# Three square weight products take their weight sums from DRAM, made earlier, and load their weights a turn at a time

## The chip, the cores and the metric

One Trainium2 chip, one core of it. The time is device microseconds (us) of one execution; the median over the runs shown is the number to predict. Engines are TensorE (PE, its weight loads PEld), VectorE (DVE), ScalarE (ACT), GpSimd (POOL) and SyncE (SP), whose queue issues nearly all DMA transfers in the order in which they stand in the program.

## What is computed

One layer of an encoder on 1024 prompt and 64 sample tokens, width 1024, all in float32, cut to its steps:

```python
h  = ffn_half(x, g_ffn1, w_ffn1_gu, w_ffn1_d)
u, q, k, v = split(rmsnorm(h, g_mix) @ w_in)       # input projection
y_ssm = s5_mixer(u, ...)                           # state space scans
y_att = diff_attn(q, k, v, ...)
h  = h + concat(y_ssm, y_att) @ w_out              # square, 1024 x 1024
mk, mv = rmsnorm(mem) @ w_ck, rmsnorm(mem) @ w_cv
q  = rmsnorm(h, g_cross) @ w_cq                    # square
h  = h + softmax_attention(q, mk, mv) @ w_co       # square
y  = rmsnorm(ffn_half(h, g_ffn2, ...), g_final)
```

The new keys, values and states are outputs as well.

## The kernel before

Matrix products run as three TensorE products of a high and a low part (line 171): ScalarE makes the high part `wh` of a 128 x 512 weight tile (line 151) and a copy `q` in PSUM (152), VectorE the low part `wl` (153).

The three square products with `w_out`, `w_cq` and `w_co` (in this order) are done as a two by two block product with seven block multiplications in place of eight (Strassen's scheme in Winograd's form). A `Block` holds one such product, `square` runs it in seven turns, in the order `TURNS = (0, 1, 3, 4, 5, 2, 6)`. A turn is 96 matmuls of 272 columns into eight banks. While turn n runs on TensorE, `prepare` gets the operands of turn n+1 ready, four times (k = 0 to 3): the split of a weight tile, a difference of activations (`value`, lines 422 and 426), and their split (450 on ScalarE, 451 on VectorE). Turns 0, 1 and 5 multiply by blocks of the weight as they are; turns 3, 4, 2 and 6 by sums and differences of blocks, which GpSimd makes in place out of the loaded blocks: three operations of 128 x 512 in `mix` (lines 433, 434, 435) for each k, and one more in `prepare` (448):

```python
G.tensor_tensor(out=s1, in0=a21, in1=a22, op=ALU.add)
G.tensor_tensor(out=a21, in0=a11, in1=a21, op=ALU.subtract)
G.tensor_tensor(out=a11, in0=a22, in1=a21, op=ALU.subtract)
```

The same class serves the down projections of the two feed-forward parts, with five more blocks.

The input projection (about 760 to 1050 us of the span) computes twelve units of 128 columns of `w_in`. The first four feed the scans `s5_main(f, u)`, which are written as generators, put into a list `bg` and moved on one step at a time as the later units are issued (`pump_all` moves each generator of the list by one step). A scan stores its input (line 1201), loads it back in another shape (1206), runs some 160 small VectorE operations (lines 1230 to 1262: products, sums and copies of two SBUF operands, 4 to 136 elements a partition), loads its two constants and its states (1268, 1270, 1271), and feeds TensorE again (1280, 1281) and a gelu on ScalarE (1282). ScalarE's line 1338 copies key or value heads to token order.

The order of every engine's instructions is set when the program is built: the framework keeps the program order of what each engine is given, weighted by priority and by the moment at which a simulated timeline has the operands ready. Tiles come from rotating pools: `row` (36 buffers, "r"), `wr` and `ws` (`half`), four buffers each, and seven of `wh` and `wl`.

Of the kernel before, what the change touches and what calls it, by code (L numbers as in the profile page):

```python
# [10 lines left out]
F32 = mybir.dt.float32  # L11
# [3 lines left out]
ALU = mybir.AluOpType  # L15
AX = mybir.AxisListType

P = 128
# [50 lines left out]
def tile_hymba_step(ctx: ExitStack, tc: tile.TileContext, a, o):  # L69
# [9 lines left out]
    wp = ctx.enter_context(tc.tile_pool(name="wp", bufs=7))  # L79
# [26 lines left out]
    def dram(shape, name):  # L106
        return dr.tile(list(shape), F32, tag=name, name=name)

    bg = deque()
# [29 lines left out]
    def half(shape=(P, 512), dt=F32):  # L139
        return wp.tile(list(shape), dt, tag="ws", name=nm("ws"), bufs=4)  # L140
# [101 lines left out]
    class Stats:  # L242


        def __init__(self):
            self.acc = None
# [132 lines left out]
    class Block:  # L379
# [11 lines left out]
        def load(self, part, k):  # L391

            n, held = self.n, self.held
            if k >= n:
                return
            j = k + (n if part > 1 else 0)
            wj = self.w_src(j)
            if part % 2 == 0:
                u = self.u[j] = held("u", k + 2 * part, row)
                load(out=u, in_=self.u_src(j))  # L400
            elif part == 1:
                self.a11[k] = held("a11", k, lambda: wp.tile([P, 512], F32, tag="wr", name=nm("wr"), bufs=4))
                self.a21[k] = held("a21", k // 2, lambda: row([P, 2, 512]))[:, k % 2]
                halves = (wj[:, 512:1024], wj[:, 0:512]) if self.swap else (wj[:, 0:512], wj[:, 512:1024])
                load(out=self.a11[k], in_=halves[0])
                load(out=self.a21[k], in_=halves[1])
            else:
                both = held("both", k, lambda: row([P, 2, 512]))
                self.a12[k], self.a22[k] = both[:, 0], both[:, 1]
                if self.swap:  # L410
                    for c in range(2):
                        load(out=both[:, c], in_=wj[:, 512 - 512 * c:1024 - 512 * c])
                else:
                    load(out=both, in_=wj.rearrange("p (c m) -> p c m", c=2))

        def value(self, q, k, late):

# [19 lines left out]
        def prepare(self, q, k, late=False):  # L437
            held = self.held
            if k == 0:
                held.turn[1] += 1  # L440
            if k >= self.n:
                return
            if self.s1[k] is None and q:
                self.mix(k)
            w = (self.a11[k], self.a12[k], self.s1[k], self.a11[k], self.a21[k], self.a22[k], self.a12[k])[q]
            self.w[q, k] = held.split_w(w)
            if q == 1:
                G.tensor_tensor(out=w, in0=w, in1=self.a11[k], op=ALU.subtract)
            v, r = self.value(q, k, late), held("x", 4 * (held.turn[1] % 2) + k, lambda: row([P, 2, HT], F32R))
            A.copy(r[:, 0], v)  # L450
            V.tensor_tensor(out=r[:, 1], in0=v, in1=r[:, 0].bitcast(F32), op=ALU.subtract)  # L451
            self.x[q, k] = r

        def product(self, q, i):

            p = [bank(), bank()]
            items = []
            for k in range(self.n):
                (wh, wl), r = self.w[q, k], self.x[q, k]
                items.append((wh[:, i * P:(i + 1) * P], wl[:, i * P:(i + 1) * P], r[:, 0], r[:, 1]))  # L460
            mm3(p, items, self.n, HC)
            return p

    TURNS = (0, 1, 3, 4, 5, 2, 6)

# [2 lines left out]
    def square(d, outs, done, step=lambda n, i: None, src_d=None):  # L468
# [19 lines left out]
        for n, q in enumerate(TURNS):  # L488
            for i in range(4):
                if q != 1:  # L490
                    residual(q, i)
                p = d.product(q, i)
                g, u = outs[i], outs[4 + i]
# [15 lines left out]
                step(n, i)  # L509
                if n < 6:  # L510
                    d.prepare(TURNS[n + 1], i, True)
                if n in (0, 2, 3, 4):
                    fetch((1, None, 5, 6, 2)[n], i)

# [831 lines left out]
    for f in range(4):  # L1346
        u = in_unit(f, True)
        pump_all()
        bg.append(s5_main(f, u))
    kT, qT, vt, vsr = [], [], [], row([NS, 4, P])  # L1350
    for hd in range(4):
        k = in_unit(8 + hd)
# [288 lines left out]
            if m % 8 == 7:  # L1641
                bg.append(subln(heads[m // 8]))

    def weights_of(w):
        return lambda k: w[k * P:(k + 1) * P]

    def begin(d):
        for k in range(4):
            d.load(1, k)
        for k in range(4):  # L1650
            d.prepare(0, k)
        for k in range(4):
            d.load(3, k)


    h2_d = dram([KT, P, NT], "h2_d")
# [40 lines left out]
    _, mv = mem_proj(a["w_cv"][0], "mem_v_prompt")  # L1697
    for t in range(2):
        store(out=mv_d[t], in_=mv[t])
    d = Block(Held(), 4, weights_of(a["w_out"][0]), cat)  # L1700
    begin(d)
    pump(1000)

# [72 lines left out]
    q = deque()  # L1776
# [9 lines left out]
                q.append(c_scores(0, i - 4 + C_EARLY))  # L1786

    bg.append(cache_prep())
    d = Block(Held(), 4, weights_of(a["w_cq"][0]), h2, swap=True)
    begin(d)  # L1790
    square(d, cq[4:] + cq[:4], lambda m, c: None, cq_step)
    pump(1000)
# [57 lines left out]
                c_values(*q.popleft())  # L1850
    while q:
        c_values(*q.popleft())
    d = Block(Held(), 4, weights_of(a["w_co"][0]), oc)
    begin(d)
    h3_d, h3 = dram([KT, P, NT], "h3_d"), [row() for _ in range(KT)]
    norm3 = Normed(h3, g_ffn2)
# [122 lines left out]
```

## Time and profile before

| | us |
|---|---|
| median of three runs | 2416.04 |
| lowest, highest | 2413.63, 2422.79 |
| the profiled execution | 2419.82 |
| its span | 2418.0 |
| PE busy | 2266.6 (94%) |
| PEld busy | 2200.5 (91%) |
| DVE busy | 1667.8 (69%) |
| ACT busy | 1308.6 (54%) |
| POOL busy | 1096.5 (45%) |
| moved by DMA | 262.64 MB |

TensorE is busy 94% of the span: the time is its work and its stalls. A busy TensorE does not run at its peak at all times: the granted clock is 1.2 GHz instead of 2.4 GHz in some short stretches, and an instruction takes twice as long there. The stages have different limits, so the questions of this change are read from two stages: the input projection with the scans, and the square products.

### The profile page before, as it was taken

What the parts mean: (1) busy time and instruction counts of PE and PEld (TensorE: products, weight loads), DVE (VectorE), ACT (ScalarE), POOL (GpSimd) and SP (SyncE); (2) the same over time, 40 slices, a digit from 0 to 9 for tenths busy, and PEclk for the clock granted to TensorE, in tenths of its full rate; (3) what the DMA queues carried; (4) which work ended last, traced back from release to release, by engine and by line L of the source; (5) the groups of instructions that cost most, each with busy time, mean ns of one, the idle gap of its engine ahead of it and who ended that gap; (6) DMA issues with size and microseconds to landing.
All of it is one profiled execution on the core that took longest, in us unless ns stands there. A gap on an engine that the chain in (4) does not pass through costs nothing. (4 is left out here: it accounts for less than half of the span.)

```text
span 2418.0 us, 45389 instructions
## 1 busy us (share of the span) xinstructions
PE 2266.6 (94%) x16914; PEld 2200.5 (91%) x16914; DVE 1667.8 (69%) x3732; ACT 1308.6 (54%) x2538; POOL 1096.5 (45%) x823
## 2 busy tenths in 40 slices
PE   6899999999999997989999899988999999998998
PEld 6799999998999997977799899888999999998997
DVE  6557543358898697259978678787654544479897
ACT  6554445446545422258856767666655444564543
POOL 2666777744144300025434420356776666644340
PEclk9999999999999998999999999999999999999999
DMA  6232444443412435533353411133232222262312
GB/s 210 71 113 81 112 114 119 118 169 144 144 40 84 145 90 142 161 122 97 108 179 125 155 62 47 61 111 98 81 99 72 75 78 81 78 221 85 115 46 92
DMA packets 267239, 262.64 MB, mean 109 GB/s; under 512 B 36445, under 2 KB 216714, under 8 KB 267018
## 3 DMA queue, kind: packets, MB, share of 16 engines
q1 hardware_dynamic: 266928, 259.72, 33.9%
q8 instruction: 133, 2.18, 0.4%
q14 instruction: 88, 0.72, 0.1%
q10 hardware_dynamic: 90, 0.02, 0.0%
HBM read 186.51 MB, written 68.58 MB: 105 GB/s over the span
## 5 line engine op out<-in xcount | busy, mean ns | idle before, releaser
L171 PE MATMUL b<-r,wh 128*128 128x272 f32 (+4 forms) x9600 | 1689.0, 296 | 68.7 <-DVE r L724 22.5
L171 PEld LDWEIGHTS b<-r,wh 128*128 128x128 f32 x9600 | 1420.9, 191 | 86.1 <-DVE r L724 26.7
L171 PE MATMUL b<-r,wl 128*128 128x272 f32 (+4 forms) x4800 | 1054.9, 295 | 23.6 <-DVE wl L153 23.6
L171 PEld LDWEIGHTS b<-r,wl 128*128 128x128 f32 x4800 | 784.6, 191 | 27.5 <-DVE wl L153 27.3
L596 DVE TENSOR_TENSOR r<-b,r 128x272 f32<-128x272 f32 x440 | 172.1, 433 | 253.2 <-PE b L171 229.1
L152 ACT CAST q<-wr 128x512 fp32r<-128x512 f32 x304 | 180.0, 592 | 269.1 <-DVE wl L153 267.0
L153 DVE TENSOR_TENSOR wl<-wr,q 128x512 fp32r<-128x512 f32 x304 | 206.8, 680 | 169.3 <-issue 69.9
L151 ACT CAST wh<-wr 128x512 fp32r<-128x512 f32 x304 | 187.9, 622 | 239.8 <-PE b L171 212.4
L451 DVE TENSOR_TENSOR r<-r,r 128x544 fp32r<-128x544 f32 x224 | 214.0, 973 | 23.9 <-ACT r L450 23.3
L433 POOL TENSOR_TENSOR ws<-r,r 128x512 f32<-128x512 f32 x32 | 54.2, 1700 | 304.4 <-DVE ws L1799 124.6
L151 ACT CAST wh<-ws 128x512 fp32r<-128x512 f32 x158 | 98.0, 620 | 134.6 <-PE b L171 113.9
L153 DVE TENSOR_TENSOR wl<-ws,q 128x512 fp32r<-128x512 f32 x158 | 107.5, 680 | 88.1 <-PE b L171 52.8
L152 ACT CAST q<-r 128x512 fp32r<-128x512 f32 x146 | 86.6, 593 | 124.5 <-DVE wl L153 124.2
L450 ACT CAST r<-r 128x544 fp32r<-128x544 f32 x224 | 144.2, 652 | 9.2 <-DMA r<-hid_d 7.6
L724 DVE SCALAR_TENSOR_TENSOR r<-b,r 128x272 f32<-128x272 f32 (+4 forms) x328 | 132.2, 437 | 21.9 <-PE b L171 20.9
L152 ACT CAST q<-ws 128x512 fp32r<-128x512 f32 x158 | 93.7, 593 | 87.1 <-DVE wl L153 82.3
L646 POOL TENSOR_TENSOR r<-r,r 128x544 f32<-128x544 f32 x44 | 61.5, 1398 | 171.7 <-DVE r L596 128.4
L1398 POOL CAST r<-r 64x256 fp32r<-64x256 f32 x32 | 13.6, 424 | 252.1 <-PE b L137 239.7
L153 DVE TENSOR_TENSOR wl<-r,q 128x512 fp32r<-128x512 f32 x146 | 99.4, 681 | 38.1 <-ACT q L152 37.1
L659 POOL TENSOR_TENSOR r<-r,r 128x1088 f32<-128x1088 f32 x44 | 111.8, 2543 | 8.8 <-ACT r L658 8.8
L137 PE MATMUL b<-ident,r 128*128 128x128 f32 (+4 forms) x649 | 93.7, 281 | 21.2 <-DMA r<-g_subln 10.6
L151 ACT CAST wh<-r 128x512 fp32r<-128x512 f32 x146 | 90.2, 620 | 42.7 <-PE b L171 29.3
(330 smaller groups left out, 2999.9 us busy)
## 6 DMA issues: line engine op xcount, KB each, us to landing
wr<-w_ffn_gu SPq DMA_DIRECT2D x194, 256.0 KB, 2.9
hid_d<-r SPq DMA_DIRECT2D x44, 544.0 KB, 2.8
r<-hid_d SPq DMA_DIRECT2D x44, 544.0 KB, 6.4
h_d<-r SPq DMA_DIRECT2D x48, 272.0 KB, 2.8
r<-h_d SPq DMA_DIRECT2D x48, 272.0 KB, 3.0
r<-w_ffn_d SPq DMA_DIRECT2D x24, 512.0 KB, 6.7
wr<-w_in SPq DMA_DIRECT2D x32, 256.0 KB, 2.7
wr<-w_ffn_d SPq DMA_DIRECT2D x20, 256.0 KB, 2.8
```

The costliest lines, as they stand in the source:

```text
L137: T.transpose(out, in_, ident[:n, :n])
L151: A.copy(hi, x)
L152: A.copy(r, x)
L153: V.tensor_tensor(out=lo, in0=x, in1=r.bitcast(F32), op=ALU.subtract)
L171: T.matmul(pc[:, :c1 - c0], w, x[:, c0:c1], start=(first + i == 0 and q == 0), stop=(first + i == n - 1 and q == 2))
L433: G.tensor_tensor(out=s1, in0=a21, in1=a22, op=ALU.add)
L450: A.copy(r[:, 0], v)
L451: V.tensor_tensor(out=r[:, 1], in0=v, in1=r[:, 0].bitcast(F32), op=ALU.subtract)
L596: V.tensor_tensor(out=oc, in0=pc, in1=tc_, op=ALU.add)
L646: G.tensor_tensor(out=gate[:, T2], in0=gate[:, T2], in1=up[:, T2], op=ALU.add)
L659: G.tensor_tensor(out=up, in0=up, in1=gate, op=ALU.mult)
L724: V.scalar_tensor_tensor(out=hc_, in0=pc, scalar=0.5, in1=hc_, op0=ALU.mult, op1=ALU.add)
```

## The change

A new DRAM tensor `sums_d` takes the four sums and differences of the blocks of `w_out`, `w_cq` and `w_co`. A generator `weight_sums` makes them: 24 tiles (three weights, four k, two halves), each with two loads of 256 KB, four GpSimd operations of 128 x 256 and one store of 512 KB. All 24 are put into `bg` behind the first scan of the input projection. The new class `SquareBlock` has no `mix`: `fetch` loads the weights of one turn, three turns ahead, from the weight itself or from `sums_d`, into three groups of buffers (`ws`, `wr` and rows) that rotate.

```diff
+    def weight_sums(n, w, swap=False):
+        i11, i21, i12, i22 = (1, 0, 3, 2) if swap else (0, 1, 2, 3)
...
+        for k in range(4):
+            for c in range(2):
+                t = row([P, 4, 256])
+                for h in range(2):
+                    wj = w[(4 * h + k) * P:(4 * h + k + 1) * P].rearrange("p (h c n) -> p h c n", h=2, c=2)
+                    load(out=t[:, 2 * h:2 * h + 2], in_=wj[:, :, c])
+                yield
+                a11, a21, a12, a22 = (t[:, i] for i in (i11, i21, i12, i22))
+                G.tensor_tensor(out=a22, in0=a21, in1=a22, op=ALU.add)
+                G.tensor_tensor(out=a21, in0=a11, in1=a21, op=ALU.subtract)
+                G.tensor_tensor(out=a11, in0=a22, in1=a11, op=ALU.subtract)
+                G.tensor_tensor(out=a12, in0=a12, in1=a11, op=ALU.subtract)
+                store(out=sums_d[n, k, c], in_=t)
...
+    class SquareBlock(Block):
...
+        def fetch(self, n, k):
+            if n >= 7:
+                return
+            q, g = TURNS[n], n % 3
+            if g < 2:
+                t = self.held("wr" if g else "ws", k, (lambda: wp.tile([P, 512], F32, tag="wr", name=nm("wr"), bufs=4))
+                              if g else lambda: half([P, 512]))
+            else:
+                t = self.held("w2", k // 2, lambda: row([P, 2, 512]))[:, k % 2]
+            if q in (0, 1, 5):
+                j, h = (k if q == 0 else 4 + k), (q == 5) != self.swap
+                load(out=t, in_=self.wd[j * P:(j + 1) * P, 512 * h:512 * h + 512])
+            else:
+                i = {2: 3, 3: 0, 4: 1, 6: 2}[q] ^ self.swap
+                load(out=t.rearrange("p (c n) -> p c n", c=2),
+                     in_=sums_d[self.number, k, :, :, i].rearrange("c p n -> p c n"))
+            self.raw[q, k] = t
+
+        def prepare(self, q, k, late=False):
+            if k == 0:
+                self.held.turn[1] += 1
+            self.w[q, k] = self.held.split_w(self.raw[q, k])
+            self.operand(q, k, late)
...
                 if n < 6:
                     d.prepare(TURNS[n + 1], i, True)
+                d.fetch(n + 3, i)
...
         bg.append(s5_main(f, u))
+        if f == 0:
+            bg.append(chain(weight_sums(0, a["w_out"][0]), weight_sums(1, a["w_cq"][0], True), weight_sums(2, a["w_co"][0])))
...
     def begin(d):
-        for k in range(4):
-            d.load(1, k)
-        for k in range(4):
-            d.prepare(0, k)
-        for k in range(4):
-            d.load(3, k)
+        for n in range(3):
+            for k in range(4):
+                d.fetch(n, k)
+            if n == 0:
+                for k in range(4):
+                    d.prepare(0, k)
```

In the built program, GpSimd's rows between the last of line 255 (end of the feed-forward part) and the attention's masks (1398) held nothing before:

```order
L255 TENSOR_TENSOR r_9481<-r_9481,r_9640 128x1088
L255 TENSOR_TENSOR r_9481<-r_9481,r_9672 128x1088
L255 TENSOR_TENSOR r_9481<-r_9481,r_9704 128x1088
L1398 CAST r_12596<-r_10629 64x256
L1400 MEMSET r_12596 64x256
```

Now all 96 sums stand there (lines 477 to 480, four to a tile; where two tiles are in hand they alternate):

```order
L255 TENSOR_TENSOR r_9482<-r_9482,r_9705 128x1088
L477 TENSOR_TENSOR r_9915<-r_9915 128x256
L478 TENSOR_TENSOR r_9915<-r_9915 128x256
L479 TENSOR_TENSOR r_9915<-r_9915 128x256
L480 TENSOR_TENSOR r_9915<-r_9915 128x256
L477 TENSOR_TENSOR r_9963<-r_9963 128x256
L478 TENSOR_TENSOR r_9963<-r_9963 128x256
L479 TENSOR_TENSOR r_9963<-r_9963 128x256
```

The 96 operations have come in between; the 48 operations of lines 433, 434, 435 and 448 that belonged to the three square products are gone further down in GpSimd's order (those of the feed-forward parts stay).

In SP's queue, ahead of the first scan's load of its states (line 1268, now 1320), stood before:

```order
L144 DMA wr_11642<-w_in 128x4x128
L1342 DMA o_new_attn_k_prompt<-r_10446 128x8x128
L1343 DMA o_attn_k_sample<-r_10447 64x128
L144 DMA wr_11795<-w_in 128x4x128
L144 DMA wr_11803<-w_in 128x4x128
L144 DMA wr_11940<-w_in 128x4x128
L144 DMA wr_11948<-w_in 128x4x128
L1268 DMA r_11023<-r_10767 64x4x136 x4
L1270 DMA r_11028<-m_d 128x1024
```

Now the loads (474) and stores (481) of the sums stand between the loads of `w_in` (144):

```order
L474 DMA r_10736<-w_cq 128x2x256 x2
L474 DMA r_10865<-w_cq 128x2x256 x2
L144 DMA wr_11951<-w_in 128x4x128
L144 DMA wr_11959<-w_in 128x4x128
L481 DMA sums_d<-r_10736 128x1024
L481 DMA sums_d<-r_10865 128x1024
L474 DMA r_10978<-w_cq 128x2x256 x2
L144 DMA wr_12112<-w_in 128x4x128
L481 DMA sums_d<-r_10978 128x1024
L144 DMA wr_12120<-w_in 128x4x128
L1320 DMA r_11115<-r_10843 64x4x136 x4
L1322 DMA r_11120<-m_d 128x1024
```

Each pair of loads and each store has come in among the loads of `w_in`, and a store waits there for GpSimd's four operations. Of the 24 stores, three stand ahead of the third store of `u_d` (line 1201, now 1253), twelve ahead of the first load of the states, fifteen ahead of the third one and eighteen ahead of the fourth.

At the begin of the product with `w_co`, SP's queue held four loads of the memory's values, and behind them the second part of the weight, whose first part (into `wr`) had been issued ahead of them:

```order
L1796 DMA r_17813<-mv_d 128x1024
L1796 DMA r_17819<-mv_d 128x1024
L406 DMA r_18688<-w_co 128x512 x2
L406 DMA r_18695<-w_co 128x512 x2
L414 DMA r_18737<-w_co 128x1024
L414 DMA r_18739<-w_co 128x1024
L414 DMA r_18741<-w_co 128x1024
L414 DMA r_18743<-w_co 128x1024
L480 DMA r_18746<-h_d 128x544
```

Now the weights of turn 0 stand behind the memory's values, in the four `ws` buffers, which the cross attention's exponentials and outputs use as well:

```order
L1847 DMA r_17994<-mv_d 128x1024
L1847 DMA r_18000<-mv_d 128x1024
L505 DMA r_18920<-sums_d 128x2x256 x2
L502 DMA ws_18868<-w_co 128x512
L502 DMA ws_18870<-w_co 128x512
L502 DMA ws_18872<-w_co 128x512
L505 DMA r_18923<-sums_d 128x2x256 x2
L502 DMA ws_18874<-w_co 128x512
L505 DMA ws_18868<-sums_d 128x2x256
```

The tiles of turn 1 (`wr`) now stand ahead of the memory's values, those of turn 0 (`ws`) behind them, and those of turn 3 (`ws` again, from `sums_d`) follow at once.

## Rows read from the trace of the kernel before

**Rows 1.** Windows of the input projection: start and end in us of the span, then the length, and of each engine the busy us and, in brackets, its instructions; behind them the mean granted clock of TensorE (1.00 is 2.4 GHz, 0.50 is 1.2 GHz), the mean busy share of the DMA engines and GB/s.
```profile
820.00:840.00 20.00, 20.00 (x141) 19.58 (x140) 10.60 (x29) 5.37 (x10) 0.00 (x0) 1.00 0.50 131
840.00:860.00 20.00, 20.00 (x148) 19.36 (x148) 19.59 (x86) 4.69 (x9) 0.00 (x0) 1.00 0.51 135
...
900.00:920.00 20.00, 18.14 (x112) 17.64 (x111) 20.00 (x141) 4.54 (x8) 0.00 (x0) 1.00 0.50 143
920.00:940.00 20.00, 11.70 (x79) 11.19 (x77) 18.79 (x143) 4.11 (x6) 0.00 (x0) 0.86 0.39 114
940.00:960.00 20.00, 18.02 (x102) 18.02 (x103) 7.78 (x31) 4.84 (x9) 0.00 (x0) 0.80 0.43 115
960.00:980.00 20.00, 19.61 (x131) 19.31 (x130) 9.24 (x30) 5.32 (x10) 0.00 (x0) 1.00 0.81 228
```

**Rows 2.** The costliest VectorE groups between 840 and 935 us: line, operation, tiles, shape, count, busy us and mean ns of one, idle time before.
```profile
L1233 DVE TENSOR_TENSOR ws<-ws 128x8 f32<-128x8 f32 (+1 forms) x105 | 20.4, 211 | 0.2
L1230 DVE TENSOR_TENSOR ws<-ws,apr 128x8 f32<-128x8 f32 (+1 forms) x81 | 14.5, 185 | 0.1
...
L153 DVE TENSOR_TENSOR wl<-wr,q 128x512 fp32r<-128x512 f32 x13 | 8.8, 675 | 0.0
...
L198 DVE TENSOR_TENSOR r<-b,r 128x362 f32<-128x362 f32 (+1 forms) x12 | 6.0, 519 | 0.0
```

**Rows 3.** Waits between 900 and 950 us, all engines: who waited for whom, us in total, times, the longest.
```profile
ACT r L1338 <- DVE r L1262: 11.4, 1, 11.4
PE b L171 <- ACT r L1338: 9.7, 1, 9.7
```

**Rows 4.** All instructions of VectorE's line 1424 (in the attention, a two-input operation on one element a partition): ns shortest, median and longest, first and last start.
```profile
L1424 DVE TENSOR_TENSOR mn<-mn x32: 130/148/711, 1078.9 to 1200.3; 128x1 f32<-128x1 f32 x32
```

**Rows 5.** All tensor_tensor instructions of GpSimd's line 1399, which run beside line 1424 in the attention.
```profile
L1399 POOL TENSOR_TENSOR r<-r,r x32: 716/729/2395, 1074.2 to 1204.6; 64x256 fp32r<-64x256 f32 x32
```

**Rows 6.** The DMA queue and one kind of issue between 820 and 1040 us: packets, MB and share of 16 engines; then KB each and the median us from issue to landing.
```profile
q1 hardware_dynamic: 38493, 27.46, 45.0%
...
wr<-w_in SPq DMA_DIRECT2D x19, 256.0 KB, 2.7
```

**Rows 7.** SP's queue, in order of time: start us, us, engine, line, operation, tiles, count.
```profile
842.03 0.35 SPq L1201 DMA_DIRECT2D u_d<-r  x1
...
910.33 2.64 SPq L1268 DMA_DIRECT2D r<-r  x4
...
952.70 2.60 SPq L1268 DMA_DIRECT2D r<-r  x4
```

**Rows 8.** The three square products, 20 us at a time (columns as in rows 1): w_out 1260 to 1300, w_cq 1360 to 1400, w_co 1560 to 1600.
```profile
1260.00:1280.00 20.00, 15.79 (x103) 15.57 (x104) 14.57 (x16) 10.89 (x24) 17.26 (x13) 0.83 0.44 161
1280.00:1300.00 20.00, 16.49 (x115) 15.80 (x114) 19.27 (x31) 11.91 (x22) 6.92 (x5) 0.91 0.41 129
1360.00:1380.00 20.00, 17.18 (x128) 15.06 (x127) 12.40 (x20) 11.55 (x23) 0.00 (x0) 1.00 0.66 202
1380.00:1400.00 20.00, 14.12 (x84) 13.17 (x83) 14.57 (x24) 9.93 (x18) 15.43 (x10) 0.74 0.33 114
1560.00:1580.00 20.00, 11.35 (x89) 11.13 (x88) 20.00 (x21) 8.52 (x19) 15.41 (x8) 0.90 0.00 0
1580.00:1600.00 20.00, 17.96 (x129) 17.51 (x129) 18.77 (x31) 14.28 (x27) 10.25 (x7) 0.93 0.53 165
```

**Rows 9.** TensorE's waits in the product w_out, 1250 to 1300 us.
```profile
PE b L171 <- DVE r L1680: 3.9, 1, 3.9
PE b L171 <- DVE wl L153: 3.5, 3, 2.0
```

**Rows 10.** TensorE's waits from 1376 to 1400 us, the last of w_ck (line 1673) and the begin of w_cq (line 171).
```profile
PE b L1673 <- DVE wl L153: 3.7, 2, 1.9
PE b L171 <- ACT wh L151: 1.9, 1, 1.9
```

**Rows 11.** TensorE's waits in the product w_co, 1550 to 1600 us.
```profile
PE b L171 <- DVE wl L153: 10.7, 3, 8.7
```

**Rows 12.** VectorE in w_out from 1255 us, in order of time: start us, us, engine, line, operation, tiles, shape, count of a run of like instructions.
```profile
1256.27 6.36 DVE L426 TENSOR_TENSOR r<-r,r 128x544 f32<-128x544 f32 x4
1262.55 1.27 DVE L1680 COPY r<-b 128x512 f32<-128x512 f32 x2
```

**Rows 13.** GpSimd in the same stretch.
```profile
1258.60 1.75 POOL L433 TENSOR_TENSOR ws<-r,r 128x512 f32<-128x512 f32 x1
...
1266.18 1.29 POOL L434 TENSOR_TENSOR r<-wr,r 128x512 f32<-128x512 f32 x1
```

**Rows 14.** All of VectorE's instructions on lines 426 and 451 in the whole span: ns shortest, median, longest.
```profile
L426 DVE TENSOR_TENSOR r<-r,r x108: 708/714/1812, 530.2 to 2308.2; 128x544 f32<-128x544 f32 x108
L451 DVE TENSOR_TENSOR r<-r,r x224: 707/718/2097, 527.2 to 2356.7; 128x544 fp32r<-128x544 f32 x112
```

**Rows 15.** TensorE at the begin of w_co.
```profile
1547.90 1.08 PE L1829 MATMUL b<-r,ws 128*64 128x256 f32 x4
...
1551.40 0.34 PE L137 MATMUL b<-ident,ws 64*128 64x64 f32 x2
1551.67 0.52 PE L171 MATMUL b<-r,wh 128*128 128x272 f32 x2
```

**Rows 16.** ScalarE just behind it.
```profile
1552.43 0.62 ACT L151 CAST wh<-r 128x512 fp32r<-128x512 f32 x1
```

More of the change, by code (lines that the diff above doesn't have):

```diff
@@ L403, in load @@
                 self.a21[k] = held("a21", k // 2, lambda: row([P, 2, 512]))[:, k % 2]
-                halves = (wj[:, 512:1024], wj[:, 0:512]) if self.swap else (wj[:, 0:512], wj[:, 512:1024])
-                load(out=self.a11[k], in_=halves[0])
-                load(out=self.a21[k], in_=halves[1])
+                load(out=self.a11[k], in_=wj[:, 0:512])
+                load(out=self.a21[k], in_=wj[:, 512:1024])
             else:
@@ L409, in load @@
                 self.a12[k], self.a22[k] = both[:, 0], both[:, 1]
[L410 to L414, printed above, removed]
+                load(out=both, in_=wj.rearrange("p (c m) -> p c m", c=2))
         def value(self, q, k, late):
@@ L448, in prepare, with operand @@
                 G.tensor_tensor(out=w, in0=w, in1=self.a11[k], op=ALU.subtract)
+            self.operand(q, k, late)
+        def operand(self, q, k, late):
+            held = self.held
             v, r = self.value(q, k, late), held("x", 4 * (held.turn[1] % 2) + k, lambda: row([P, 2, HT], F32R))
@@ L462, in product, with __init__ @@
             return p
+    sums_d = dram([3, 4, 2, P, 4, 256], "sums_d")
+    def weight_sums(n, w, swap=False):
+        i11, i21, i12, i22 = (1, 0, 3, 2) if swap else (0, 1, 2, 3)
+        before = None
+        for k in range(4):
[12 more added lines that the diff above has]
+    class SquareBlock(Block):
+        def __init__(self, number, w, u, swap=False):
+            super().__init__(Held(), 4, None, u, swap=swap)
+            self.number, self.wd, self.raw = number, w, {}
+        def fetch(self, n, k):
[19 more added lines that the diff above has]
+            self.w[q, k] = self.held.split_w(self.raw[q, k])
+            self.operand(q, k, late)
     TURNS = (0, 1, 3, 4, 5, 2, 6)
@@ L1642, in tile_hymba_step @@
                 bg.append(subln(heads[m // 8]))
-    def weights_of(w):
-        return lambda k: w[k * P:(k + 1) * P]
     def begin(d):
-        for k in range(4):
-            d.load(1, k)
-        for k in range(4):
-            d.prepare(0, k)
-        for k in range(4):
-            d.load(3, k)
+        for n in range(3):
[4 more added lines that the diff above has]
+                    d.prepare(0, k)
     h2_d = dram([KT, P, NT], "h2_d")
@@ L1699, in tile_hymba_step @@
         store(out=mv_d[t], in_=mv[t])
-    d = Block(Held(), 4, weights_of(a["w_out"][0]), cat)
+    d = SquareBlock(0, a["w_out"][0], cat)
     begin(d)
@@ L1788, in tile_hymba_step @@
     bg.append(cache_prep())
-    d = Block(Held(), 4, weights_of(a["w_cq"][0]), h2, swap=True)
+    d = SquareBlock(1, a["w_cq"][0], h2, swap=True)
     begin(d)
@@ L1852, in tile_hymba_step @@
         c_values(*q.popleft())
-    d = Block(Held(), 4, weights_of(a["w_co"][0]), oc)
+    d = SquareBlock(2, a["w_co"][0], oc)
     begin(d)
```

## The prediction

> **What bounds the kernel now.** Parts 1 and 2 of the page come first: TensorE is busy 94% of the span, so a change pays by the stalls of TensorE that it removes and costs by those that it adds. Two stages matter, and the windows show both. In the product stages I read a window's loss as its length less TensorE's busy time, plus its length times what the mean granted clock lacks to 1. For w_out that gives 4.2 + 3.4 and 3.5 + 1.8, for w_cq 2.8 and 5.9 + 5.2, for w_co 8.7 + 2.0 and 2.0 + 1.4, in sum 41 us in six windows [rows 8]. The waits say by whom they end, nearly always VectorE or ScalarE behind it [rows 9 to 11].
>
> In the input projection GpSimd has nothing to do, and the windows look free [rows 1]. But VectorE is full from 840 to 940 us (19.59, 20.00 and 18.79 of 20 in the rows shown). There it works on the scans, in operations of 0.2 us [rows 2]. Where TensorE falls to 11.70 of 20, the waits give the chain: TensorE waited 9.7 us for line 1338 on ScalarE, and this 11.4 us for line 1262, the scan's last on VectorE [rows 3]. What VectorE loses before 940 us, TensorE loses too. Ahead of 840 and behind 940 us VectorE has slack (10.60 and 7.78 of 20) [rows 1].
>
> **What the change removes.** In each product 16 GpSimd operations of 128x512, 48 in all. They cost TensorE nothing themselves; what they cost is VectorE's time beside them. Lines 426 and 451 take 0.71 us alone, up to 1.8 and 2.1 beside GpSimd [rows 14]; four of line 426 took 6.36 us where 2.6 would do [rows 12], while GpSimd stretched from 1.29 to 1.75 us [rows 13]. Behind these four stands line 1680, for which TensorE waited 3.9 us. So the price of the mixing is read product by product.
>
> - w_out: waits 3.9 + 3.5 [rows 9], clock 5.2 [rows 8], in sum 12.6. Part of the clock's loss has other gaps behind it. I take 11.
> - w_cq: waits 3.7 + 1.9 [rows 10], clock 5.2, in sum 10.8. The first half of the 3.7 belongs to w_ck's own weight loads and stays. I take 8.
> - w_co: the longest wait, 8.7 [rows 11], clock 3.4, in sum 12.1. Small waits are left. I take 11.
>
> In sum 30 us; the bounds are 15 (VectorE is at 20.00 and 19.27 of 20 there and may stay the limit by its own work) and 41 (all that is lost in the six windows).
>
> **What it adds in the products.** Each loads 28 tiles of 256 KB in place of 16, 3.1 MB more. DMA engines were busy 0.00 to 0.66 there [rows 8], and weights now come three turns ahead: nothing, as long as a turn takes longer than four loads. At w_co there is no such lead. The four `ws` buffers of turn 0 are held by the cross attention: lines 1829 and 137 read them until 1548.98 and 1551.74, and TensorE began the product at 1551.67, with weights that SP had issued ahead of the memory's values [rows 15]. Now the last tile is loaded from 1551.74, lands 2.7 us later (a load of the same size, [rows 6]), and is split in 0.62 us for line 151 [rows 16], as much again for line 152, and 0.68 for line 153 [rows 2]: ready at 1556.3, 4.7 us after the old begin. The first is ready at 1548.98 + 2.7 + 1.9 = 1553.6, 1.9 late, and TensorE can work on what it has. I take 4 us.
>
> **What it adds in the input projection.** 96 GpSimd operations of 128x256. Before, none of this length ran beside the scans, so the price is bounded by the nearest row. In the attention line 1424, a one-element VectorE operation with two operands in SBUF, takes 0.148 us as a rule and 0.711 at most [rows 4], beside line 1399 on GpSimd, which also has 256 elements a partition and takes 0.72 us [rows 5]. So a GpSimd operation holds VectorE for up to 0.711 - 0.148 = 0.56 us. The lower bound is nothing, for one that meets an operation that reads PSUM, as lines 153 and 198 do (8.8 and some 6 us of the 95 that rows 2 cover).
>
> The Trainium skill ("SBUF — State Buffer", section "Who interferes with whom") has it as a rule: a VectorE instruction with two SBUF inputs contends with a GpSimd instruction that reads SBUF, over a pair of ports that they share as an exclusive lock. Rows 4 and 14 agree. Were each blocked for GpSimd's whole instruction, it would be 0.72 us in place of 0.56, and the term below 35 in place of 27.
>
> How many fall into the full stretch? By SP's order three tiles of 24 are stored ahead of a store that ran at 842.03, and fifteen ahead of one that ran at 952.70 [rows 7]. So twelve tiles, 48 operations, 48 x 0.56 = 27 us. This makes the full stretch longer by about as much, and three more tiles fall into it: 60 x 0.56 = 34. About one in five will meet an operation that takes no second SBUF operand: 27. The last six and the first three tiles lie in VectorE's slack and cost nothing; without that cover they would be 36 x 0.56 = 20 us. TensorE pays the 27 in full, since it already waits for the scan, and its clock falls longer after a longer pause; the pause of 9.7 us stands beside 2.8 + 4.0 us lost to the clock [rows 1], so I add 3. In sum 30 us, bounds 8 and 60 (96 x 0.56, plus 6 for the clock).
>
> The DMA's part: 24 tiles bring 1 MB each, 25 MB. From 820 to 1040 us 27.46 MB took 45.0% of 220 us, 99 us [rows 6]; 25 MB more are 91 us, together 190 of 220. It fits, but with little air. A store stands in SP's queue until GpSimd has made its tile, and `w_in`'s and the scans' loads stand behind it. `w_in` is loaded about two units ahead, which hides waits of a few us. I take nothing, and a rival takes the rest.
>
> **The sum.** -30 + 4 + 30 = +4 us. The profiled execution took 2419.82, 3.8 above the median of 2416.04; the difference is put on the median: 2420 us, no change that could be told (0.5%, about 12 us, is the least that a measurement of this kernel can tell from nothing).
>
> **The rivals.**
>
> - The sums are hidden. For it: TensorE has weights ahead until 900 us (20.00 of 20, [rows 1]) and GpSimd could be pressed into the gaps of VectorE, which starts one of its small operations every 0.14 us (143 in 20 us). Against it: rows 4 and 3. The cost would be 8, the net -30 + 4 + 8 = -18, or 2398. From a cost of 14 downwards the kernel is faster by over 0.5%. Chance 0.22.
> - The lock takes all. All 96 operations are paid, since the full stretch moves on with the delay and the sums with it, with the whole 0.56 and the clock: 60 - 26 = +34, or 2450. Midway, with 80 operations and no credit for PSUM, 45 + 4 - 26 = +23, or 2439. It decides from a cost of 38 upwards. For it: rows 1, where VectorE has not a tenth of slack for 100 us. Against it: its slack from 940 us on. This ends on the slower side. Chance 0.22.
> - The queue. Stores that wait for GpSimd hold up loads on the scans' path. Six stores stand between the first and the fourth scan's load of states; if each holds the queue for its tile's four operations, 4 x 0.72 = 2.9 us [rows 5], on top of the sum: +4 + 17 = +21, or 2437. For it: the order of SP, and the 190 of 220 us. Against it: a landing took 2.7 us and the pace of `w_in` is slow. Chance 0.13.
> - The products give back only half, 15 us, as VectorE stays full in them without GpSimd: +4 + 15 = +19, or 2435. This is the change not doing what it says. Chance 0.08.
> - My sum, between -8 and +12: chance 0.35.
>
> **How the numbers follow.** The predicted time is that of the sum, 2420, its own range 2408 to 2430. Faster by over 0.5%: the first rival, and a little of the sum's lower end, 0.23. Slower: 0.22 + 0.13 + 0.08 less what of these stays below +12, plus the sum's upper end, 0.37. The same: 0.40. To leave out no more than two in ten, the range goes from the first rival's 2397 to between the second one's midway and its full price, 2446.
>
> **What would show it.** Right, if the windows of 1260 to 1300, 1380 to 1400 and 1560 to 1580 in the new profile show TensorE's loss down to 2 to 4 us in each, lines 426 and 451 near 0.72 us, and the windows from 860 to 980 some 30 us more of TensorE's waits, on line 1338 or the scans, beside lines 1230 to 1262 that take up to 0.7 us. Wrong in the first way, if the scan's operations stay at 0.2 us and the wait for line 1262 at 11 us; in the second, if VectorE is full until 1000 us; in the third, if TensorE's waits end on DMA loads of `w_in` or of states; in the fourth, if VectorE is at 19 and more of 20 in the products and TensorE still waits for lines 153 and 1680. The 4 us at w_co show as a wait for line 151 or 153 at its begin.

## The result and the profile after

The changed kernel takes 2433.41 us (median; 2430.04 to 2435.42), the kernel before 2416.95 us in the same comparison. The ratio is 1.0063, with a 95% interval of 1.005 to 1.0077: the change makes it slower by some 15 us, just past what a measurement can tell. The forecast was 2420 us and no change that can be told; the range, 2397 to 2446, holds the time.

The head of the page after:

```profile
span 2430.3 us, 45664 instructions
PE 2271.2 (93%) x16914; PEld 2202.0 (91%) x16914; DVE 1670.9 (69%) x3732; ACT 1306.9 (54%) x2538; POOL 1087.5 (45%) x871
```

The engines do nearly the same work as before. TensorE's order is nearly the same too, so its n-th instruction can be matched in both traces. How much later it starts in the second is a delay that tells where time went, and from here on a step is the change of that delay over a stretch (us, from one profiled execution of each kernel; stretches by the time in the kernel before):

| stretch | 0-839 | 839-963 | 963-1038 | 1247-1351, w_out | 1351-1442, w_cq | 1442-1526 | 1526-1565, w_co begins | 1565-1592 | 1592-end |
|---|---|---|---|---|---|---|---|---|---|
| changed | -1.0 | +24.9 | +7.4 | -10.7 | -6.5 | -1.3 | +6.8 | -9.9 | +2.6 |

The sum is +12.2 (rounded parts). Between 1038 and 1247 us nothing changes. From 0 to 839 us, where next to nothing was changed, the runs below that leave this stretch alone have steps between -3.9 and +2.0: so much is scatter there.

In the input projection, the windows of the changed kernel (columns as in rows 1) answer to [rows 1]:

```profile
840.00:860.00 20.00, 19.24 (x142) 18.34 (x140) 19.57 (x71) 3.53 (x7) 5.85 (x8) 1.00 0.89 283
860.00:880.00 20.00, 15.14 (x86) 14.65 (x87) 20.00 (x97) 3.36 (x7) 7.56 (x10) 0.83 0.78 241
880.00:900.00 20.00, 16.31 (x106) 15.29 (x105) 20.00 (x116) 4.44 (x9) 4.99 (x8) 0.83 0.46 150
900.00:920.00 20.00, 19.93 (x122) 19.49 (x122) 20.00 (x87) 3.50 (x6) 8.94 (x12) 1.00 0.39 129
920.00:940.00 20.00, 16.97 (x91) 16.46 (x90) 20.00 (x139) 5.54 (x9) 3.93 (x5) 0.83 0.74 227
940.00:960.00 20.00, 10.96 (x54) 10.46 (x53) 17.71 (x106) 1.81 (x4) 5.59 (x8) 0.75 0.71 226
960.00:980.00 20.00, 12.95 (x78) 12.95 (x79) 9.03 (x32) 3.83 (x8) 0.86 (x2) 0.74 0.30 95
980.00:1000.00 20.00, 17.42 (x117) 16.78 (x116) 8.63 (x30) 3.68 (x7) 5.95 (x9) 1.00 0.90 261
```

VectorE is now full into the window from 940 on (17.71 where it was 7.78), and gets through fewer operations: 71 from 840 and 87 from 900 us, where there were 86 and 141 [rows 1]. From 960 us on it has slack again; from 980 us the DMA engines are at 0.90. The scan's costliest VectorE group of rows 2, now line 1285, between 840 and 960 us:

```profile
L1285 DVE TENSOR_TENSOR ws<-ws 128x8 f32<-128x8 f32 (+1 forms) x110 | 26.8, 258 | 0.5
```

It takes 258 ns where it took 211 [rows 2]. Line 153, which takes one of its two operands from PSUM, kept its duration (679 ns beside 675). The waits between 925 and 968 us show the chain of [rows 3] again (line 1390 was 1338, line 1314 was 1262):

```profile
ACT r L1390 <- DVE r L1314: 18.2, 1, 18.2
PE b L171 <- ACT r L1390: 12.2, 1, 12.2
```

The products gave back nearly what they should: windows of w_out, w_cq and w_co (the last after its begin; answering to [rows 8], later by the delay) have GpSimd at 0.00 and the clock at 1.00. TensorE is nearly full in w_out and w_co, and lacks 3.4 us in w_cq.

```profile
1280.00:1300.00 20.00, 20.00 (x165) 20.00 (x164) 16.94 (x28) 11.78 (x27) 0.00 (x0) 1.00 0.65 227
1400.00:1420.00 20.00, 16.64 (x128) 15.85 (x129) 12.10 (x28) 12.21 (x24) 0.00 (x0) 1.00 0.50 166
1580.00:1600.00 20.00, 19.68 (x157) 19.46 (x156) 18.32 (x33) 15.50 (x33) 0.00 (x0) 1.00 0.43 150
```

And VectorE's line 426, now 421, takes its shortest time throughout the three products (line 451, now 450, still has a few operations of up to 1.89 us). First line 426 before, from 1247 to 1600 us, then line 421 after, from 1278 to 1610:

```profile
L426 DVE TENSOR_TENSOR r<-r,r x48: 709/716/1812, 1251.3 to 1583.1; 128x544 f32<-128x544 f32 x48
L421 DVE TENSOR_TENSOR r<-r,r x48: 707/719/727, 1281.9 to 1593.2; 128x544 f32<-128x544 f32 x48
```

### The profile page after: what moved, and what is told of

Read it like the earlier page. It is cut to its first block, busy times and chain, and to the rows that moved or that the text cites. A ratio compares the mean times of both kernels' runs of the same rounds, so it can differ in the third digit from the quotient of the medians.

```text
span 2430.3 us, 45664 instructions
## 1 busy us (share of the span) xinstructions
PE 2271.2 (93%) x16914; PEld 2202.0 (91%) x16914; DVE 1670.9 (69%) x3732; ACT 1306.9 (54%) x2538; POOL 1087.5 (45%) x871
## 5 line engine op out<-in xcount | busy, mean ns | idle before, releaser
L450 DVE TENSOR_TENSOR r<-r,r 128x544 fp32r<-128x544 f32 x224 | 203.9, 929 | 23.9 <-ACT r L449 22.8
L153 DVE TENSOR_TENSOR wl<-ws,q 128x512 fp32r<-128x512 f32 x182 | 124.0, 681 | 103.3 <-PE b L171 52.2
L151 ACT CAST wh<-ws 128x512 fp32r<-128x512 f32 x182 | 112.6, 620 | 140.8 <-PE b L171 113.3
L588 POOL TENSOR_TENSOR r<-r,r 128x544 f32<-128x544 f32 x28 | 40.6, 1449 | 294.0 <-ACT r L587 293.5
L152 ACT CAST q<-ws 128x512 fp32r<-128x512 f32 x182 | 107.8, 592 | 101.0 <-DVE wl L153 95.3
L698 POOL TENSOR_TENSOR r<-r,r 128x544 f32<-128x544 f32 x44 | 61.4, 1396 | 172.5 <-DVE r L648 135.6
L152 ACT CAST q<-r 128x512 fp32r<-128x512 f32 x122 | 72.3, 593 | 114.1 <-DVE wl L153 114.1
L137 PEld LDWEIGHTS b<-ident,r 128*128 128x128 f32 (+4 forms) x649 | 76.8, 147 | 35.0 <-DMA r<-x_prompt 11.0
L153 DVE TENSOR_TENSOR wl<-r,q 128x512 fp32r<-128x512 f32 x122 | 83.1, 682 | 28.6 <-ACT q L152 27.0
L668 POOL TENSOR_TENSOR ws<-wr,wr 128x512 f32<-128x512 f32 x44 | 60.8, 1382 | 87.2 <-DMA wr<-w_ffn_gu 66.5
```

The costliest lines, as they stand in the source:

```text
L137: T.transpose(out, in_, ident[:n, :n])
L151: A.copy(hi, x)
L152: A.copy(r, x)
L153: V.tensor_tensor(out=lo, in0=x, in1=r.bitcast(F32), op=ALU.subtract)
L668: G.tensor_tensor(out=s1, in0=r[2], in1=r[3], op=ALU.add)
L698: G.tensor_tensor(out=gate[:, T2], in0=gate[:, T2], in1=up[:, T2], op=ALU.add)
```

## The experiments

### What the input projection pays for

Theory A: GpSimd's operations hold VectorE while the scans run. Theory B: the 25 MB and the stores in SP's queue are the cost. Four runs leave out one of the two, or both.

`no_sums_math` takes the four operations out:

```diff
-                G.tensor_tensor(out=a22, in0=a21, in1=a22, op=ALU.add)
-                G.tensor_tensor(out=a21, in0=a11, in1=a21, op=ALU.subtract)
-                G.tensor_tensor(out=a11, in0=a22, in1=a11, op=ALU.subtract)
-                G.tensor_tensor(out=a12, in0=a12, in1=a11, op=ALU.subtract)
                 store(out=sums_d[n, k, c], in_=t)
```

> The changed kernel without the four GpSimd operations of each sums tile: loads and stores stay, so what reaches sums_d is not the sums, and the output is wrong. Theory A (VectorE is held by GpSimd's reads while the scans run): TensorE's delay at the end of the input projection, 32 us in the changed kernel, falls to 8 us or less, time 2405 to 2412 us. Theory B (the 25 MB and the stores in SP's queue are the cost): the delay stays at 25 us or more, time 2425 us or more. Both in part: between them, and the share of each is read from the delay.

Measured: 2409.36 us, against 2417.12 for the kernel before in this comparison (0.9961, 0.9946 to 0.9975). The step of 839-963 falls from +24.9 to +3.6, that of 963-1038 stays, +7.8 for +7.4. So 21 us of the first step are GpSimd's operations, and some 11 us of the whole are not. What the operations did to VectorE is read from the scan's five groups of small operations between 840 and 960 us. First the changed kernel (with line 1285 above), then this one (its line numbers are smaller by four):

```profile
L1284 DVE TENSOR_TENSOR ws<-ws,api 128x4 f32<-128x4 f32 (+1 forms) x86 | 18.9, 220 | 0.0
L1282 DVE TENSOR_TENSOR ws<-ws,apr 128x8 f32<-128x8 f32 (+1 forms) x85 | 18.8, 223 | 0.3
L1283 DVE TENSOR_TENSOR ws<-ws,apn 128x4 f32<-128x4 f32 (+1 forms) x86 | 17.1, 199 | 0.0
L1301 DVE TENSOR_TENSOR ws<-ws,r 128x8 f32<-128x8 f32 x68 | 13.4, 200 | 0.2
```

```profile
L1281 DVE TENSOR_TENSOR ws<-ws 128x8 f32<-128x8 f32 (+1 forms) x114 | 23.3, 218 | 0.4
L1280 DVE TENSOR_TENSOR ws<-ws,api 128x4 f32<-128x4 f32 (+1 forms) x91 | 15.6, 173 | 0.0
L1278 DVE TENSOR_TENSOR ws<-ws,apr 128x8 f32<-128x8 f32 (+1 forms) x90 | 17.5, 195 | 0.2
L1279 DVE TENSOR_TENSOR ws<-ws,apn 128x4 f32<-128x4 f32 (+1 forms) x91 | 15.6, 172 | 0.0
L1297 DVE TENSOR_TENSOR ws<-ws,r 128x8 f32<-128x8 f32 x68 | 11.2, 168 | 0.2
```

Count times the difference of the means, over the five groups, is 15 us. In the changed kernel GpSimd makes 48 operations in this stretch, each of its four lines as many as this one:

```profile
L477 POOL TENSOR_TENSOR r<-r 128x256 f32<-128x256 f32 x12 | 9.4, 784 | 74.2 <-DMA r<-w_out 26.9 <-DVE ws L1285 16.5 <-DMA r<-w_cq 15.8
```

That is about 0.32 us of VectorE for one operation of GpSimd.

`memset_sums` puts operations of nearly the same length in their place that write but read nothing:

```diff
+                for i in range(4):
+                    G.memset(t[:, 2 * (i % 2):2 * (i % 2) + 2], 1.0)
```

> The four GpSimd operations of a tile are replaced by four memsets of 128x512, which write and read nothing (the sums are left out, the output is wrong). Loads and stores stay. If only GpSimd's reads hold VectorE (theory A as the Trainium skill's page on SBUF has it), the time is that of the kernel without these operations within 4 us, and the scan's operations keep their 0.2 us. If any GpSimd operation on SBUF holds it, or if the stores that wait for GpSimd are what costs (theory B), the time is near the changed kernel's, 2425 to 2434 us.

Measured: 2408.89 us (0.9964, 0.9948 to 0.9979), not to be told from the former; the steps are +5.1 and +7.6. The memsets did run, in a group of GpSimd between 820 and 1060 us:

```profile
L478 POOL MEMSET r<- 128x512 f32 x96 | 48.6, 527 | 172.9 <-DMA r<-w_out 58.6 <-DMA r<-w_cq 46.0 <-DMA r<-w_co 45.0
```

And the scan's group (line 1283 in this kernel) kept its duration:

```profile
L1283 DVE TENSOR_TENSOR ws<-ws 128x8 f32<-128x8 f32 (+1 forms) x115 | 23.8, 222 | 0.4
```

222 ns stand beside 258 in the changed kernel and 218 with no operation of GpSimd at all. 96 memsets of 0.53 us on GpSimd cost VectorE next to nothing; the stores waited for them as they did for the sums, though for less time, as a sum took about 0.76 us. This is what the rule weighed in the prediction says (the Trainium skill, "SBUF — State Buffer", "Who interferes with whom"), that an instruction that only writes doesn't contend, and this trace agrees. A memset differs in more than its reads, though: it is shorter and has no operands.

`no_store` leaves out the stores (half of the added bytes) and keeps the operations.

```diff
-                store(out=sums_d[n, k, c], in_=t)
...
-                     in_=sums_d[self.number, k, :, :, i].rearrange("c p n -> p c n"))
+                     in_=self.wd[k * P:(k + 1) * P, 0:512].rearrange("p (c n) -> p c n", c=2))
```

> The sums are made but not stored (24 stores of 512 KB are left out); the square products read the first block of the raw weight in their place, the same bytes in the same tiles, so the output is wrong. Theory A: 22 to 28 us of the 32 us delay stay, time 2423 to 2431 us. Theory B: the delay falls to less than 15 us, time below 2417 us.

Measured: 2429.46 us (1.0044, 1.003 to 1.0058). The steps are +20.5 and +10.2. The stores alone are not the cost; the operations are its larger part. Behind 963 us the loss is there without any store, and with half of the added bytes.

`no_sums` is the change without `weight_sums` at all: only the products are new.

```diff
-        if f == 0:
-            bg.append(chain(weight_sums(0, a["w_out"][0]), weight_sums(1, a["w_cq"][0], True), weight_sums(2, a["w_co"][0])))
```

> Only the square products of the change: the sums, their loads and their stores are left out, and the products read the first block of the raw weight where they would read sums (the output is wrong). If the input projection's 32 us are 22 for VectorE held by GpSimd and 10 for the transfers, as the run without GpSimd's operations has it (2409 us), the time is 2397 to 2402 us and TensorE's delay at the end of the input projection is 0. If those 10 us have another cause, the time stays near 2409 us.

Measured: 2397.05 us, against 2419.66 (0.9903, 0.9888 to 0.9918). Both steps of the projection are gone (-0.6 and +0.8); the products keep theirs. So the change's gain is 23 us. By the profiles (-23.6 here, +12.2 in the changed kernel) the sums cost 36: 21 for the reads of GpSimd, some 11 for what is left of the sums without them (transfers, places in the queue, buffers), 2 of the late begin of w_co (+4.9 here), and 2 in small steps.

What the transfers do is seen in the queue's row of the changed kernel from 820 to 1060 us, beside [rows 6]:

```profile
q1 hardware_dynamic: 54213, 53.01, 71.1%
...
wr<-w_in SPq DMA_DIRECT2D x19, 256.0 KB, 3.9
```

The same loads land after 3.9 us instead of 2.7, and the window from 980 us on, with the DMA engines at 0.90, is one in which a scan fetches its states and constants. In `no_sums_math` two of TensorE's waits from 965 to 1055 us end on loads:

```profile
PE b L1328 <- DMA r<-m_d: 2.4, 1, 2.4
PE b L1328 <- DMA wr<-w_in: 2.2, 1, 2.2
```

In `no_store` the largest is another one there: 5.6 us in two waits for line 1392 on VectorE, which waited 11.3 us for GpSimd's line 480, the last to use a tile of sums. Which part of the 11 us is landing, place in the queue or buffers held by the tiles was not taken apart.

### Is the place the fault?

`in_ffn1` hands the sums to the generator that prepares the scans in the first feed-forward part:

```diff
-*(s5_prep(f) for f in range(4))), ORDERED, on_row=mix_row)
+*(s5_prep(f) for f in range(4)), weight_sums(0, a["w_out"][0]), weight_sums(1, a["w_cq"][0], True),
+    weight_sums(2, a["w_co"][0])), ORDERED, on_row=mix_row)
```

> The same sums, made in the first feed-forward part behind the preparation of the scans, instead of during the input projection. VectorE is busy about 5 tenths there and GpSimd about 6 to 7. Theory A: the cost of 32 us goes, and the new place costs 0 to 8 us, as VectorE has slack to be held in: time 2400 to 2410 us, faster than the kernel before. Theory B: the DMA engines are busy 2 to 4 tenths there, so it would cost little as well; this run tells nothing between A and B but whether the place is the fault. If holding VectorE costs the same wherever it is done, the time stays at 2425 us or more.

Measured: 2448.31 us (1.0118, 1.0095 to 1.0142), a clear miss. The projection's cost is gone (steps -1.5 and -0.5), but 48 us are lost between 480 and 608 us, 44 of them from 536 us on. The generator is emptied at the end of the gate and up products, so the sums came all at once:

```profile
540.00:560.00 20.00, 8.00 (x45) 7.17 (x43) 18.74 (x16) 4.79 (x12) 20.00 (x17) 0.67 1.01 361
560.00:580.00 20.00, 8.90 (x48) 8.72 (x48) 1.90 (x4) 2.30 (x4) 20.00 (x30) 0.57 1.03 412
```

GpSimd and the DMA engines are full there. The waits from 536 to 605 us say what TensorE stood still for:

```profile
PE b L171 <- ACT wh L151: 23.3, 2, 21.1
ACT wh L151 <- DMA r<-w_ffn_d: 19.4, 2, 19.3
ACT wh L151 <- POOL ws L428: 9.0, 2, 8.2
```

The longest one ends on the loads of the down projection's weights, which stand among those of the sums in SP's queue; the mixing (line 428), which stands behind the sums on GpSimd, comes second.

`ffn1_down` spreads them: into `bg` ahead of that part, a tile at every third step of the down projection.

```diff
+                yield
+                yield
                 yield
...
+    bg.append(chain(weight_sums(0, a["w_out"][0]), weight_sums(1, a["w_cq"][0], True), weight_sums(2, a["w_co"][0])))
     ffn(ops0, a["w_ffn1_gu"][0], ...
```

> The sums are made during the down projection of the first feed-forward part, one tile at every third step of its blocks, instead of during the input projection; the run that put them there all at once cost 50 us in one place. VectorE is busy 14 to 16 of 20 us there, GpSimd 6 to 9, the DMA engines between a quarter and full. If what costs is a VectorE with no slack, the cost of 32 us falls to 5 to 12 us: time 2402 to 2413 us. If each operation costs what it holds VectorE wherever it is (96 x 0.56 = 54 us), the time is above 2430 us.

Measured: 2453.26 us (1.0135, 1.012 to 1.015), again a miss. The reason is not the lock on its own. At 600 us GpSimd was full, with the mixing of this part and the sums behind one another. TensorE waited for line 449 on ScalarE (450 before), and this for a row buffer that a tile of sums held until its store:

```profile
600.00:620.00 20.00, 9.36 (x65) 9.14 (x63) 18.63 (x23) 6.08 (x11) 20.00 (x16) 0.76 0.15 52
```

```profile
PE b L171 <- ACT r L449: 21.6, 2, 14.0
ACT r L449 <- DMA sums_d<-r: 18.3, 2, 10.9
```

The first fence is the window, the second the waits of TensorE and ScalarE from 600 to 650 us. By the steps 27 us are lost from 536 to 700 us, 17 more from there to 839, and 9 at the begin of the second feed-forward part; the last two were not taken apart. `ffn1_down_co`, the same with the edit of the next section:

> Both edits: sums in the down projection of the first feed-forward part, and w_co's turn 0 in wr. If they are independent, it is 4 to 7 us less than with the first alone: time 2396 to 2408 us, faster than the kernel before and than the changed one.

Measured: 2450.85 us (1.0125, 1.011 to 1.014); the expected 2396 to 2408 fell with its base. The step of w_co's begin is 0.0 here too.

### The late begin of w_co

`co_wr` rotates the buffer groups of w_co by one, so that turn 0 lies in `wr`:

```diff
-            q, g = TURNS[n], n % 3
+            q, g = TURNS[n], (n + (self.number == 2)) % 3
```

> The changed kernel; for w_co alone the three groups of buffers rotate by one, so turn 0 is loaded into wr, which is free early, turn 1 into the rows and turn 2 into ws. If the late begin of w_co (6.8 us in the trace of the changed kernel) comes of ws being held by the cross attention, 4 to 7 us of it go: time 2426 to 2430 us. If it comes of something else (the split behind other work), the time stays at 2431 to 2435 us.

Measured: 2440.68 us (1.0087, 1.0069 to 1.0106), slower than the changed kernel. The cause of the late begin is shown all the same: the step of +6.8 is 0.0 here. But the begin of the second feed-forward part loses 11.0 us where it lost 1.1: more loads of its weights into `wr` came to stand in SP's queue ahead of the loads whose blocks GpSimd mixes (line 662), fourteen instead of twelve, and loads there wait for free buffers. That this is the cause is argued here; `split1` and `split2` below test the same place.

### After the scans

`after_scans` starts the sums behind the first key unit:

```diff
-        if f == 0:
-            bg.append(chain(weight_sums(0, ...
...
         bg.append(to_tokens(k, row([P, 8, P]), row([NS, P]), "new_attn_k_prompt", "attn_k_sample", hd))
+        if hd == 0:
+            bg.append(chain(weight_sums(0, a["w_out"][0]), weight_sums(1, a["w_cq"][0], True), weight_sums(2, a["w_co"][0])))
```

> The changed kernel with the sums begun four units later, behind the first key unit of the input projection: by SP's order four tiles in place of twelve are stored ahead of the first scan's load of states, eight in place of eighteen ahead of the fourth. If VectorE without slack is the cost, it falls from 22 us by the share of tiles moved into the slack behind 940 us, to 7 to 13 us; the transfers cost about 10 as before. Time 2416 to 2426 us. If the cost does not hang on where VectorE is full, the time stays at 2430 us or more.

`split` also moves the eight tiles of w_co into the cross attention:

```diff
+    co_sums = weight_sums(2, a["w_co"][0])
     for hd in range(4):
         for i in range(9):
+            if i % 3 == 0:
+                next(co_sums, None)
             if hd or i >= C_EARLY:
```

> As the former, with the eight tiles of w_co made in the cross attention instead (one at every third step), where GpSimd has nothing to do, the DMA engines are busy 0.00 to 0.08 from 1485 to 1545 us and VectorE 16 of 20. If slack is what counts, these 32 operations cost 0 to 4 us there and the transfers of the input projection a third less: time 2411 to 2422 us. If the cross attention's chain of small operations on VectorE is what TensorE waits for, the 32 x 0.56 = 18 us are paid there, and the time is above 2425 us.

Measured: 2430.36 us (1.0048, 1.003 to 1.0066) and 2428.97 us (1.0046, 1.0029 to 1.0063), both above what was expected. A third of the tiles was left in the full stretch, but the step of 839-963 fell only to +19.4 and +23.0. The waits of `split` from 925 to 968 us name what had come in:

```profile
ACT r L1390 <- DMA sums_d<-r: 27.0, 1, 27.0
PE b L171 <- ACT r L1390: 22.0, 1, 22.0
```

Line 1390 was waiting for the row buffer that it writes: a tile of sums held it until its store, which ran at 957.66, behind loads that were issued at 950.41. A buffer shared between the two is a third way to pay for the sums, the one that `ffn1_down` had shown at line 449. By the code the wait of [rows 3] was for a buffer as well: line 1338 copies a PSUM bank into a row tile and reads nothing of the scan, so what tied it to line 1262 is the row buffer of the scan's `x`, which that line reads last. Whether another pool for these copies would take the wait away was not tried. The cross attention charged nothing: the steps of `split` there are within 1.5 us of the changed kernel's.

`split1` starts w_out's and w_cq's tiles one key unit later, behind the scans (`if hd == 1`):

> As the run before (w_co's sums in the cross attention), but the sixteen tiles of w_out and w_cq begin behind the second key unit, three units later: by SP's order none is stored ahead of the second load of states, one ahead of the third. If what is left of the cost is VectorE's full stretch and the row buffers that sums tiles hold until they are stored while the scans need buffers, TensorE's delay at 960 us falls from 19 us to 3 or less and at the end of the input projection from 27 to 8 to 12 (the transfers): time 2405 to 2413 us, faster than before. If sums tiles hold up ScalarE's copies (line 1390) wherever they stand in the projection, the delay stays above 20 us and the time above 2420 us.

Measured: 2417.06 us (0.9991, 0.9982 to 1.0), above the expected 2405 to 2413. As expected the step of 839-963 is gone (-0.1) and that of 963-1038 stays (+7.7). But +9.0 came up at the begin of the second feed-forward part, in the same place as in `co_wr`. The waits there, 1660 to 1700 us:

```profile
ACT wh L151 <- POOL r L668: 10.1, 1, 10.1
PE b L171 <- ACT wh L151: 6.3, 1, 6.3
```

and SP's queue in order of time:

```profile
1649.25 27.62 SPq L144 DMA_DIRECT2D wr<-w_ffn_gu  x6
1676.92 2.15 SPq L662 DMA_DIRECT2D r<-w_ffn_gu  x4
```

`split2` steps the tiles of w_co two positions later, which restores the order of that place:

```diff
-            if i % 3 == 0:
+            if i % 3 == 2:
                 next(co_sums, None)
```

> The run before lost 8 us anew at the begin of the second feed-forward part: there one load into wr, which waits for its buffer, had come to stand in SP's queue ahead of the four loads of the blocks that GpSimd mixes (line 662), and these ran at 1676.9 while TensorE stood still for 6.4 us. With the tiles of w_co made two steps later in the cross attention (i % 3 == 2 in place of 0) the order of that place is the changed kernel's again, twelve loads into wr ahead of line 662 instead of thirteen. If that one place was the loss, the time is 2407 to 2412 us, faster than the kernel before; if the 8 us have another cause, it stays at 2414 us or more.

Measured: 2407.89 us, against 2418.53 (0.9953, 0.9939 to 0.9967). It is faster than the kernel before by some 11 us and than the changed one by some 25 (from two comparisons). One load fewer stands in the way:

```profile
1647.54 20.75 SPq L144 DMA_DIRECT2D wr<-w_ffn_gu  x5
1668.38 2.11 SPq L662 DMA_DIRECT2D r<-w_ffn_gu  x4
```

and the step of 1656-1764 us is +1.1. In the projection this kernel loses nothing from 839 to 963 us and 9.2 us from 963 to 1038; this and w_co's begin (+5.1) are the largest losses left. The 9.2 us are not transfers alone: from 963 to 1060 us line 1390 waits 5.5 us for buffers that tiles of sums hold until their store.

## Why the prediction was right, point by point

The range holds the time, but the forecast of no change that can be told does not: 2433 us lie 13 us above 2420, and above the sum's own 2408 to 2430. What follows takes the terms one by one.

- **The products.** -11, -8, -11 were forecast for w_out, w_cq, w_co; -10.7, -6.5, -9.9 were measured. Reading the price off TensorE's waits and the clock in each product's own windows held to 2 us, and line 426's longest time of 1812 ns, now 727, shows the mechanism. In every kernel with this change w_out has -10.7, and w_co between -9.8 and -11.1; w_cq varies from -3.3 to -6.5. The -1.3 behind w_cq is 0.0 in `co_wr`, so it is not this product's.
- **w_co's late begin.** +4 was forecast, +6.8 measured; that it comes of the `ws` buffers is shown by `co_wr` (0.0). TensorE's waits from 1563 to 1575 us are for the splits of the late tiles:

```profile
PE b L171 <- DVE wl L153: 2.0, 1, 2.0
PE b L171 <- ACT wh L151: 0.9, 1, 0.9
```

These are 2.9 us, less than the 4. The rest is the clock, for which this term had nothing: the granted clock was 0.83 from 1555 to 1575 us, which lacks 3.4 us, where it was 1.00 at the begin of w_co before.

```profile
1555.00:1565.00 10.00, 9.31 (x34) 6.40 (x35) 4.51 (x13) 5.76 (x15) 0.00 (x0) 0.83 0.21 70
1565.00:1575.00 10.00, 6.86 (x36) 5.90 (x35) 10.00 (x18) 6.30 (x13) 0.00 (x0) 0.83 0.35 115
```

- **The input projection.** +30 was forecast, +32.3 measured, but the total is right by luck: three sizes were wrong, and the errors cancel.
  - The hold of VectorE was forecast as 60 operations x 0.56 us, a fifth off, so 27. The 48 operations of twelve tiles came (the row of line 477 has GpSimd waiting for loads in more than half of its idle time, which held the other tiles back), and one cost VectorE 0.32 us, which makes 15. The 0.56 was the longest hold of one row, taken for all.
  - The clock was forecast as 3. By the starts and ends of TensorE's matched instructions, 14.9 of the +24.9 us are standing still and 9.9 are slower matmuls; in `no_sums_math` it is 3.6 and 0.0. So of the 21 us that GpSimd's operations cost, some 11 are waits and some 10 the clock: the windows above lack 20 us to the full clock from 840 to 980 us, where 6.8 were lacking [rows 1]; part of that falls into the pauses.
  - For the transfers nothing was forecast, and some 11 us are left without GpSimd's operations. The failed step is "I take nothing, and a rival takes the rest". The rival of the queue, with its 17 us, was nearer in size and came beside the lock, not instead of it; but its mechanism, stores that wait for GpSimd, is not needed, since the step behind 963 us is +10.2 without stores.
- **What the prediction left out.** +2.6 us came up behind 1592 us, in the second feed-forward part, where the change touches nothing; it is +1.7 in `no_sums`, and its cause is open. `split1` and `split2` show that the order in SP's queue at its begin can cost 8 us there.
- The first rival, hidden sums, is refuted by the scan's 258 ns; the second, all 96 operations paid, by the step of 21 us and by VectorE's 9.03 of 20 from 960 us on; the fourth, half the gain, by the products' steps.

The sum of the measured terms is +12.2 against a forecast of +4: 2.8 of the difference at w_co's begin, 2.6 at the end, 2.3 in the projection, 2.9 in the three products, and -2.3 in the two small steps of 0-839 and 1442-1526. The medians stand 16.5 us apart, so 4 us of the miss are between the profiled executions and the medians.

## What to carry to other kernels

An engine that looks free in a stage isn't free to use there if its reads hold up the engine that is full: before moving work to GpSimd, look at whether VectorE has slack in that window, and which of its operations read two operands from SBUF (the scan's did and were held; line 153, with one in PSUM, kept its 0.68 us). Ask of moved work three things apart: whom it holds up while it runs, which queue its transfers stand in and what is behind them, and whose buffers its tiles keep until they are stored; here they cost 21 us (the lock, half of it by the clock), 8 (a place in the queue) and a wait of 22 (a buffer). A good change may need only another place: the same sums behind the scans and in the cross attention made the kernel 0.5% faster instead of 0.6% slower.

## What the runs showed of the hardware

96 GpSimd memsets of 0.53 us beside a full VectorE cost it next to nothing (222 ns beside 218 per operation of the scan), while 96 tensor_tensor operations of about 0.76 us cost 21 us of the stage: the memsets write and read nothing, and the longer operations read two operands. The hold was about 0.32 us of VectorE for each of the 48 in the full stretch, less than half of their length. Beside it, one row buffer that a sums tile held until its store stopped TensorE for 22.0 us in one piece, where it had waited 9.7 us before; and one load more that stood ahead of others in SP's queue and waited for its buffer stopped it for 6.3 us.
